# The last branch's operand kept in SBUF, the block combination moved into another stage, stores spread over three queues, and PSUM banks shared by stage

## The chip, the cores and the metric

One core of one Trainium2 chip runs the program. The metric is the device time of one execution in microseconds (us). The time before is 1762.13 us, the median of 3 runs (1758.29 to 1766.15).

A core has five engines with a queue each: PE (matmul, with its weight loads shown as PEld), DVE (vector), ACT (scalar functions), POOL and SP. They work side by side and wait for each other through semaphores; each queue is worked off in order. DMAs between the memories are started from a queue, which may have to wait there for the data that it is to store or for the buffer that it is to fill. Everything behind that DMA on the queue then waits as well. Matmuls write to PSUM, which has eight banks of 128 x 512 float32.

## The reference

One decoder block on x (1024 tokens, 1024 features), in float32: an RMSNorm, one wide projection that feeds three branches (a chunked gated delta rule, stick-breaking attention, attention on 256 memory tokens), a gated merge, an output projection with the residual, and a last RMSNorm.

```python
proj = rmsnorm(x, norm_g) @ w_in
dn_qkv, dn_z, dn_b, dn_a, sb_qkv, sb_z, m_q, m_z, gates = split(proj)
dn_qkv = silu(causal_dwconv(dn_qkv, conv_w))
o_dn = gated_delta_rule(l2norm(dq) * 128**-0.5, l2norm(dk), dv, beta, g)
o_dn = merge_heads(rmsnorm(o_dn, dn_norm_g)) * silu(dn_z)
o_sb = merge_heads(stick_breaking_attention(sq, sk, sv)) * silu(sb_z)
o_m = merge_heads(memory_attention(mq, mk, mv)) * silu(m_z)
g_dn, g_sb, g_m = split(sigmoid(gates), 3)
merged = g_dn * (o_dn @ w_br_dn) + g_sb * (o_sb @ w_br_sb) + g_m * (o_m @ w_br_mem)
out = rmsnorm(x + merged @ w_out, final_g)
```

The delta rule keeps a 128 x 128 state S for each of 8 heads; for each chunk it needs the inverse of a unit triangular matrix.

## The kernel before

**Arithmetic.** Each float32 operand of a large matmul is split into a high part (rounded by ACT) and a low part (the rest, by DVE; `split`, L136). A product is three matmuls: high·high, high·low, low·high (`mm3`, L150).

**The dense projection.** `stream` (L164) walks a list of jobs. A job is a pair of 128-feature groups for all 1024 tokens, done as a block product with seven multiplications instead of eight: units B11, B21, T1, T2, T3, B22, T4, of 12 matmuls each, 84 in all. Its four weight blocks are loaded from SP into `wb` (6 tiles); T units are differences of them, made by DVE. Each unit is split into `wu` (6 units ahead). The products gather in three kinds of bank, Y (two), X and Z (one each). A job's `evac` is called with each quarter of the result. One step of the generator, one unit, is called a *slot*, seven to a job. Slots are interleaved by hand with other work: `pacer` (L829) runs a second generator so far that its share of pieces matches the share of slots that have gone by.

**Order.** The program is written in order; the framework then plans each engine's queue by that order and by a simulated timeline, so neighbouring pieces can change places.

1. Norm (L254 to L358): x and mem are loaded, squared with a sum (ACT), scaled by the root and the gain in one DVE operation (L263), transposed by PE, split.
2. kq: eight jobs for k and q of the delta rule, four for the gate `sz`. `kq_head` (L473) convolves, and stores `kt`, `qd`, `kd`, `at`, `md`, `mo` for each half of a head; POOL masks the decay table `gam` (L482), clears the pads of `xp` (L457) and makes the row factors.
3. v (7 jobs: v and sv in turn) and z (10 jobs: mq, then dz and g in turn, mz). Beside them runs `solver` (L642), which inverts the 64 x 64 blocks on DVE: 62 elimination steps of two operations (L671, L674) on M, for all heads and chunks at once, then stores of the blocks (L680, L687). It has 80 pieces over the 119 slots of v and z. `memory` (L692) runs from z on. `stored` (L430) writes gates and z's through two staging tiles `st`.
4. Attention (L920 to L1007): `weights` makes z, two sigmoids, masks and a product scan (L942); `values` (L958) transposes and splits the weights, then multiplies by V. Between its pieces run the slots of skq and of the other eight gate jobs. `z` has one bank.
5. Merge (from L1018): `branch` (L1052) multiplies an operand with 128 columns of a branch's weights, gates the product and adds it to `mer`: first `ym` (8 times, 2 operand tiles), then `ysb` (8 times, 8 tiles). Beside these two run `combine` (L732), which joins pairs of 64-blocks into 128-blocks by two small products per head, and `recurrence` (L758), 16 steps (8 chunks, 2 groups of 4 heads) of four pieces: 80 pieces over 40 calls. A step loads kt, vb, tt, kd, qd, at; multiplies k·S (L780), T·r (L788), o = q·S + a·v (L795, L796) and dS (L800); squares, scales and transposes o; and stores it to `odn_d` in DRAM. When all are done, `load_o` (L1038) loads `odn_d` and `zf_d` tile by tile through `raw` (two tiles) and `gt`, multiplies and splits them, and `ydn` runs (8 times), with `wout` loaded beside it.
6. Output (from L1099): merged @ w_out, residual, norm, store.

All DMAs are started from SP.

Of the kernel before, what the change touches and what calls it, by code (L numbers as in the profile page):

```python
# [25 lines left out]
SV = 0.45  # L26
# [10 lines left out]
def hybrid_block(ctx, tc, x, mem, norm_g, mem_norm_g, wq, wv0, wba, convw, a_log, dt_bias,  # L37
# [39 lines left out]
    open_psum("psA", tr=4)  # L77
# [176 lines left out]
    def norm(pool_, src, g_bc, nm):  # L254
        xt = pool_.tile([P, T], F32, tag="xt", bufs=3, name="xt_" + nm)
        sy.dma_start(out=xt, in_=src)
        xn = pool_.tile([P, T], F32, tag="xn", name="xn_" + nm)
# [33 lines left out]
    def memory_kv():  # L291
        kv = [mp_.tile([P, 2, 256], F32, name=f"kv{j}") for j in range(2)]
        for i in range(2):
# [4 lines left out]
            ve.tensor_copy(kv[0][:, i, :], o[:, 0:256])  # L298
# [7 lines left out]
        ve.tensor_copy(kv[1], o.rearrange("p (a b) -> p a b", a=2))  # L306
# [114 lines left out]
    open_psum("psC", tr=2, wk=2)  # L421
# [5 lines left out]
    def staged(nm):  # L427
        return st.tile([P, 512], F32, tag="st", bufs=2, name=nm)

    def stored(d, fn, nm, post=None):  # L430

        def evac(i, j, a, b):
# [10 lines left out]
            sy.dma_start(out=d[j][:, half(i)], in_=t)  # L443
# [29 lines left out]
    def kq_head(h):  # L473
# [18 lines left out]
        def chunks(i):  # L492
# [3 lines left out]
            sy.dma_start(out=chunked(kt_d, h, i), in_=kv)  # L496
# [5 lines left out]
            sy.dma_start(out=chunked(qd_d, h, i), in_=qd)  # L502
# [3 lines left out]
            for j, (src, ss) in enumerate(((kv, ssk[:, s]), (qv, eq[:, h, s]))):  # L506
# [4 lines left out]
                if j == 0:  # L511
# [3 lines left out]
                    sy.dma_start(out=chunked(kd_d, h, i), in_=kd)  # L515
# [10 lines left out]
            sy.dma_start(out=chunked(at_d, h, i), in_=ma[:, :, 1, :])  # L526
            for b in range(2):
                q = slice(b * 64, b * 64 + 64)
                sy.dma_start(out=md_d[b, h, s].rearrange("n j i -> j n i"), in_=ma[q, :, 0, q])
            sy.dma_start(out=mo_d[h, :, s, :], in_=ma[0:64, :, 0, 64:P])  # L530
# [30 lines left out]
    def v_heads(g):  # L561
        xps = {}

        def conv(j, i):
# [8 lines left out]
            sy.dma_start(out=chunked(vb_d, h, i), in_=vb)  # L573
# [15 lines left out]
    def sv_heads(g):  # L589
        def evac(i, j, a, b):  # L590
# [6 lines left out]
            for d, s in zip(sv_d, hl):  # L597
                sy.dma_start(out=d[h, :, i * 4:i * 4 + 4, :], in_=f(s))
# [7 lines left out]

    mq = {}
# [6 lines left out]
    def gates(n):  # L614

        return (PQ_G + n, f"g{n}", stored([g_d[(2 * n + j) // 8, (2 * n + j) % 8] for j in range(2)],
                                          AF.Sigmoid, f"g{n}"))

    def silu_out(first, n, d, nm, post=None):
        return (first + n, f"{nm}{n}", stored([d[2 * n + j] for j in range(2)], AF.Silu, f"{nm}{n}", post))  # L620
# [16 lines left out]
    mzj = [silu_out(PQ_MZ, 0, zm_d, "mz", twice_silu)]  # L637
    dzj = [silu_out(PQ_DZ, n, zf_d, "dz", twice_silu) for n in range(4)]
    gj = [gates(n) for n in range(12)]


# [50 lines left out]
    def memory():  # L692
# [3 lines left out]
        for h in range(4):  # L696
# [25 lines left out]
            for hf in range(2):  # L722
# [6 lines left out]
                sy.dma_start(out=om_d[h // 2, r0:r0 + 64, half(hf)], in_=t[r0:r0 + 64])  # L729
            yield  # L730

    def combine():  # L732
        s_ = ExitStack()
        vp = pool("comb", 2, side="right", stack=s_)
# [23 lines left out]
    def recurrence():  # L758
# [9 lines left out]
        for n in range(NT):  # L768
            for g in range(2):
# [57 lines left out]
    SOLVE, MEM, RECUR = 1 + 1 + 62 + 8 + 8, 4 * 5, 16 + 16 * 4  # L827
# [21 lines left out]
    add("v", [vj[0], svj[0], vj[1], svj[1], vj[2], svj[2], vj[3]])  # L849
    add("z", mqj + [dzj[0], gj[0], dzj[1], gj[1], dzj[2], gj[2], dzj[3], gj[3]] + mzj)  # L850
# [43 lines left out]
    def beside():  # L894
        solve((pos[0] - first) / total)
# [8 lines left out]
    mem_ = pacer(memory(), MEM)  # L904
    start2 = pos[0]

    def beside2():
        beside()
        mem_((pos[0] - start2) / 60.0)
# [3 lines left out]
    solve(2.0)  # L913
    m_st.close()
    open_psum("psD", z=1, tr=2, av=1)


    d_st = sub()
    dp = pool("D", 1, stack=d_st)
# [38 lines left out]
    def values(h, i, at, vt):  # L958
# [18 lines left out]
        for b in range(i + 2):  # L977
# [3 lines left out]
            pe.matmul(o, vh, ah[:, b, cs_], start=(b == 0), stop=False)  # L981
            pe.matmul(o, vh, al_[:, b, cs_], start=False, stop=False)  # L982
            pe.matmul(o, vl, ah[:, b, cs_], start=False, stop=(b > i))
# [35 lines left out]
    opool = pool("op", 1, stack=w_st)  # L1019
    mp = pool("merged", 1, stack=w_st)  # L1020
# [17 lines left out]
    def load_o(src, ks, nm, by=None, op_=None, bufs=12):  # L1038
        res = []
        for k in ks:  # L1040
            raw = fp.tile([P, T], F32, tag="raw", bufs=2, name=f"oraw_{nm}_{k}")
            sy.dma_start(out=raw, in_=src[k])
            if by is not None:
                z_ = fp.tile([P, T], F32, tag="gt", bufs=4, name=f"oz_{nm}_{k}")
                sy.dma_start(out=z_, in_=by[k])
                ve.tensor_tensor(out=raw, in0=raw, in1=z_, op=ALU.mult)
            o = tuple((op_ or opool).tile([P, T], F32R, tag=f"o{j}", bufs=bufs, name=f"o{j}_{nm}_{k}") for j in "hl")
# [4 lines left out]
    def branch(i, w, nm, oT, br, first, each=lambda: None):  # L1052
        gt_ = fp.tile([P, T], F32, tag="gt", bufs=4, name=f"gt_{nm}")
# [157 lines left out]
```

## Time and profile before

| | us |
|---|---|
| median of 3 runs | 1762.13 |
| the profiled execution | 1764.58 |
| its span, first to last instruction | 1762.9 |

The profile's second part cuts the span into 40 slices of 44 us; a digit is the busy share in tenths, PEclk the granted TensorE clock in tenths of full speed, DMA the busy share of 16 DMA engines.

```profile
PE   4899999999979986999899999999868999729998
DVE  5887888879999952456777777767744334444332
ACT  5567877765544663644455454544422212322021
POOL 1002112110000000000101110111200001200011
PEclk9999999999999997999999999999968999959999
DMA  6336557564342244233123222311288746665122
```

The stages lie at 0 to 85 us (norm), 85 to 347 (kq), 347 to 497 (v), 497 to 775 (z), 775 to 1286 (attention), 1286 to 1575 (ym, ysb and the recurrence), 1575 to 1666 (ydn) and on to the end (output). A matmul that follows another closely starts 0.23 us after it at full clock (128 x 512), though each is shown with 0.39 us; so a busy PE need not be a PE at its peak.

### The profile page before, as it was taken

Reading aid. Unit: us, or ns where it says so; the run is one execution under the profiler, and the core shown is the slowest. Engines: PE = TensorE matmul, PEld = TensorE weight load, DVE = VectorE, ACT = ScalarE, POOL = GpSimd, SP = SyncE. Lnnn points to the kernel's source line nnn. Section 1 sums busy time; section 2 is a strip of 40 time slices with the busy share of each in tenths; the row PEclk is TensorE's granted clock in tenths of the full one; section 3 lists DMA queues with packets and bytes.
Section 4 is the critical chain, followed back from the end, with each engine's and each line's share of the span. In section 5 each row is a group of like instructions: output and inputs, shape, how many; then the busy total and the mean of one; then the engine's idle time right before and its main releaser. Section 6 shows DMA issues by size and latency. Waiting matters only on the chain.

```text
span 1762.9 us, 23066 instructions
## 1 busy us (share of the span) xinstructions
PE 1574.6 (89%) x7963; PEld 1304.6 (74%) x7963; DVE 1165.1 (66%) x1828; ACT 838.8 (48%) x1890; POOL 169.4 (10%) x405
## 2 busy tenths in 40 slices
PE   4899999999979986999899999999868999729998
PEld 4887788888867764777787778778756888628786
DVE  5887888879999952456777777767744334444332
ACT  5567877765544663644455454544422212322021
POOL 1002112110000000000101110111200001200011
PEclk9999999999999997999999999999968999959999
DMA  6336557564342244233123222311288746665122
GB/s 224 113 102 205 147 149 206 148 190 125 120 132 66 96 90 102 84 108 114 61 81 112 77 78 91 102 61 43 72 229 241 233 157 203 221 225 170 36 91 77
DMA packets 181317, 228.27 MB, mean 129 GB/s; under 512 B 50768, under 2 KB 104272, under 8 KB 181072
## 3 DMA queue, kind: packets, MB, share of 16 engines
q1 hardware_dynamic: 181200, 226.80, 41.7%
q8 instruction: 63, 1.03, 0.3%
q14 instruction: 54, 0.44, 0.1%
HBM read 152.72 MB, written 74.02 MB: 129 GB/s over the span
## 4 chain that ended last, share of the span: by engine, by line
PE 71%; DVE 11%; DMA 7%; ACT 4%; issue 3%; SPq 2%; POOL 1%; DVEq 0%; POOLq 0%; ACTq 0%
PE mmY_g L154 2%; PE mmY_g L155 2%; PE mmY_g L156 2%; PE y_ysb L1061 2%; PE y_ysb L1063 2%; PE y_ysb L1062 2%; PE y_ydn L1061 2%; PE mmY_skq L154 2%; PE out L1119 2%; PE y_ydn L1062 2%; PE mmY_skq L156 2%; PE mmY_skq L155 2%; PE out L1117 2%; PE y_ydn L1063 2%; PE out L1118 2%
## 5 line engine op out<-in xcount | busy, mean ns | idle before, releaser
L942 DVE TENSOR_TENSOR_SCAN pf<-pf 128x512 f32<-128x512 f32 (+4 forms) x96 | 98.3, 1024 | 38.0 <-POOL pf L940 35.4
L1061 PE MATMUL y_ydn<-oh_dn,wh_ydn 128*128 128x512 f32 x128 | 50.9, 398 | 38.0 <-ACT wh_ydn L1033 38.0
L137 ACT ACTIVATE aTh<-aTp 128x512 fp32r<-128x512 f32 (+2 forms) x96 | 45.1, 496 | 55.0 <-PE aTp L968 49.0
L936 ACT ACTIVATE pf<-z 128x512 f32<-128x512 f32 (+4 forms) x96 | 46.5, 485 | 48.5 <-PE z L156 48.1
L982 PE MATMUL av<-aTl,vh 128*128 128x256 f32 (+1 forms) x160 | 48.5, 303 | 12.6 <-DVE aTl L138 12.6
L138 DVE TENSOR_TENSOR aTl<-aTp,aTh 128x512 fp32r<-128x512 f32 (+2 forms) x96 | 50.8, 541 | 12.8 <-ACT aTh L137 12.8
L138 DVE TENSOR_TENSOR wu_g_T<-wt_g_T,wu_g_T 128x512 fp32r<-128x512 f32 x48 | 33.1, 689 | 36.4 <-ACT wu_g_T L137 36.3
L1061 PEld LDWEIGHTS y_ydn<-oh_dn,wh_ydn 128*128 128x128 f32 x128 | 24.6, 192 | 43.6 <-ACT wh_ydn L1033 38.4
L945 DVE TENSOR_TENSOR pf<-be,pf 128x512 f32<-128x512 f32 (+4 forms) x96 | 53.4, 556 | 4.0
L1061 PE MATMUL y_ysb<-oh_sb,wh_ysb 128*128 128x512 f32 x128 | 52.0, 407 | 2.9 <-ACT wh_ysb L137 2.9
L674 DVE TENSOR_TENSOR M<-M,tmp 128x62 f32<-128x62 f32 (+30 forms) x62 | 52.7, 850 | 0.3
L671 DVE TENSOR_TENSOR tmp<-M 128x62 f32<-128x62 f32 (+30 forms) x62 | 52.7, 850 | 0.3
L1117 PE MATMUL out<-oh_wo,mh 128*128 128x512 f32 x128 | 50.3, 393 | 1.8 <-ACT mh L137 1.8
L1062 PE MATMUL y_ysb<-ol_sb,wh_ysb 128*128 128x512 f32 x128 | 51.6, 403 | 0.0
L1063 PE MATMUL y_ysb<-oh_sb,wl_ysb 128*128 128x512 f32 x128 | 51.5, 404 | 0.0
L1062 PE MATMUL y_ydn<-ol_dn,wh_ydn 128*128 128x512 f32 x128 | 50.6, 395 | 0.0
L1063 PE MATMUL y_ydn<-oh_dn,wl_ydn 128*128 128x512 f32 x128 | 50.3, 395 | 0.0
L1118 PE MATMUL out<-ol_wo,mh 128*128 128x512 f32 x128 | 50.3, 393 | 0.0
L1119 PE MATMUL out<-oh_wo,ml 128*128 128x512 f32 x128 | 49.7, 392 | 0.0
L154 PE MATMUL z<-kh,qh 128*128 128x512 f32 (+4 forms) x96 | 36.6, 381 | 14.3 <-ACT be L937 14.3
L940 POOL TENSOR_SCALAR_AFFINE_SELECT pf<-pf 128x128 f32<-128x128 f32 x64 | 22.8, 356 | 273.7 <-ACT pf L936 270.9
L137 ACT ACTIVATE wu_g_T<-wt_g_T 128x512 fp32r<-128x512 f32 x48 | 30.1, 630 | 38.7 <-PE mmY_g L156 11.9
(790 smaller groups left out, 5379.3 us busy)
## 6 DMA issues: line engine op xcount, KB each, us to landing
wb_g_b<-in_wq_dram SPq DMA_DIRECT2D x48, 256.0 KB
g_d<-g SPq DMA_DIRECT2D x48, 256.0 KB
wb_kq_b<-in_wq_dram SPq DMA_DIRECT2D x32, 256.0 KB
wb_skq_b<-in_wq_dram SPq DMA_DIRECT2D x32, 256.0 KB
xt_x<-in_x_dram SPq DMA_DIRECT2D x8, 512.0 KB
wb_sz_b<-in_wq_dram SPq DMA_DIRECT2D x16, 256.0 KB
kt_d<-kq SPq DMA_DIRECT2D x16, 256.0 KB
gam<-gr_d SPq DMA_DIRECT2D x8, 512.0 KB
```

The source lines that it names most:

```text
L137: sc.activation(dst[0], src, AF.Copy)
L138: ve.tensor_tensor(out=dst[1], in0=src, in1=f(dst[0]), op=ALU.subtract)
L154: pe.matmul(o, ah, bh, start=(first and i == 0), stop=False, **kw)
L155: pe.matmul(o, ah, bl, start=False, stop=False, **kw)
L156: pe.matmul(o, al, bh, start=False, stop=(i == n - 1), **kw)
L942: ve.tensor_tensor_scan(out=pv[:, ::-1], data0=pv[:, ::-1], data1=pv[:, ::-1], initial=pf[:, off + c1:off + c1 + 1], op0=ALU.mult, op1=ALU ...
L1061: pe.matmul(oo[hf], wh[:, k, :], oh[:, s], start=(k == 0), stop=False)
L1062: pe.matmul(oo[hf], wh[:, k, :], ol[:, s], start=False, stop=False)
L1063: pe.matmul(oo[hf], wl[:, k, :], oh[:, s], start=False, stop=(k == n - 1))
L1117: pe.matmul(oo[hf], mh[:, k, :], wo[k][0][:, s], start=(k == 0), stop=False)
L1118: pe.matmul(oo[hf], mh[:, k, :], wo[k][1][:, s], start=False, stop=False)
L1119: pe.matmul(oo[hf], ml[:, k, :], wo[k][0][:, s], start=False, stop=(k == KC - 1))
```

## The change

- *The last branch's operand.* The recurrence loads `zt`, its part of silu(dn_z), multiplies the transposed o with it and splits it into `odn`, two SBUF tensors of 128 x 8 x 1024. `odn_d`, its stores and loads go. To make room, `kd`, `qd`, `at` have one buffer instead of two, the branch weights two instead of three, the gates are loaded by halves into two half tiles (four whole ones before), operands have 8 buffers (12), and `om`'s multiplier goes through `raw`.
- *Combine.* It runs in z, from 72% of the slots of v and z to 98%, after the solver, whose pieces are spread over those 72%; it has single buffers.
- *Jobs.* v: v and g in turn (four each), then three sv. z: mq, four dz, mz. `memory` is spread over 32 slots instead of 60. The first four gates are made with tanh on ACT and a POOL operation.
- *Queues.* On ACT: kt, sz, vb, om, gates from the fifth on. On POOL: qd, kd, at, md, mo, sv, dz, mz, the first four gates. Staging has three tiles.
- *Banks.* X has a bank of its own only in kq, v and z; in attention it shares two banks with z. The norm has five banks for transposes.
- *Norm.* POOL multiplies by the gain, ACT scales by the root.
- *Attention.* `values` begins with the blocks whose weights were split first. Three slots run between `memory` and the first attention piece.

```diff
-    MM = dict(Y=2, X=1, Z=1)
+    MM = dict(Y=2, Z=1)
     def psum(tag, name):
+        if tag == "X" and "X" not in banks["tags"]:
+            tag = "z"
...
         sc.activation(xn, xt, AF.Square, accum_out=ss)
+        gp.tensor_tensor(out=xt, in0=xt, in1=g_bc, op=ALU.mult)
...
-        ve.scalar_tensor_tensor(out=xt, in0=xt, scalar=rs, in1=g_bc, op0=ALU.mult, op1=ALU.mult)
-        return xt
+        sc.activation(xn, xt, AF.Copy, scale=rs)
+        return xn
...
-    open_psum("psC", tr=2, wk=2)
+    open_psum("psC", tr=2, wk=2, X=1)
...
-            sy.dma_start(out=d[j][:, half(i)], in_=t)
+            q.dma_start(out=d[j][:, half(i)], in_=t)
...
-            sy.dma_start(out=chunked(qd_d, h, i), in_=qd)
+            gp.dma_start(out=chunked(qd_d, h, i), in_=qd)
...
+    def sigmoid(t, src, nm):
+
+        sc.activation(t, src, AF.Tanh, scale=0.5)
+        gp.tensor_scalar(out=t, in0=t, scalar1=0.5, scalar2=0.5, op0=ALU.mult, op1=ALU.add)
...
-                kd = ld(kd_d, n, g, "kd") if n < NT - 1 else None
-                qd = ld(qd_d, n, g, "qd") if n else None
-                at = ld(at_d, n, g, "at")
+                kd = ld(kd_d, n, g, "kd", 1) if n < NT - 1 else None
+                qd = ld(qd_d, n, g, "qd", 1) if n else None
+                at = ld(at_d, n, g, "at", 1)
+                zt = ep.tile([P, 4, P], F32, tag="zt", bufs=1, name=f"zt_{n}_{g}")
+                sy.dma_start(out=zt, in_=zf_d[g * 4:g * 4 + 4, :, n * P:n * P + P].rearrange("h d t -> d h t"))
...
-                os_ = ep.tile([P, 4, P], F32, tag="os", bufs=2, name=f"os_{n}_{g}")
-                sc.activation(os_, o.rearrange("p (h c) -> p h c", h=4), AF.Copy)
-                sy.dma_start(out=odn_d[g * 4:g * 4 + 4, :, n * P:n * P + P].rearrange("h d c -> d h c"), in_=os_)
+                ve.tensor_tensor(out=zt, in0=o.rearrange("p (h c) -> p h c", h=4), in1=zt, op=ALU.mult)
+                split([t[:, g * 4:g * 4 + 4, n * P:n * P + P] for t in odn], zt)
...
-    add("v", [vj[0], svj[0], vj[1], svj[1], vj[2], svj[2], vj[3]])
-    add("z", mqj + [dzj[0], gj[0], dzj[1], gj[1], dzj[2], gj[2], dzj[3], gj[3]] + mzj)
+    add("v", [vj[0], gj[0], vj[1], gj[1], vj[2], gj[2], vj[3], gj[3]] + svj)
+    add("z", mqj + dzj + mzj)
...
     def beside():
-        solve((pos[0] - first) / total)
+        solve((pos[0] - first) / (SF * total))
...
-        mem_((pos[0] - start2) / 60.0)
+        mem_((pos[0] - start2) / 32.0)
+        if pos[0] - first > SF * total:
+            solve(2.0)
+            comb((pos[0] - first - SF * total) / ((0.98 - SF) * total))
...
-    open_psum("psD", z=1, tr=2, av=1)
     d_st = sub()
     dp = pool("D", 1, stack=d_st)
+    for _ in range(3):
+        slot()
+    open_psum("psD", z=2, tr=2, av=1)
...
-        for b in range(i + 2):
+        bs = list(range((i + 1) // 2 if i >= 4 else 0, i + 2)) + (list(range((i + 1) // 2)) if i >= 4 else [])
+        for m, b in enumerate(bs):
...
-    recur = pacer(itertools.chain(combine(), recurrence()), RECUR)
+    recur = pacer(recurrence(odn), RECUR)
...
-        w = [fp.tile([P, T], F32R, tag=f"w{j}", bufs=3, name=f"w{j}_{nm}") for j in "hl"]
+        w = [fp.tile([P, T], F32R, tag=f"w{j}", bufs=2, name=f"w{j}_{nm}") for j in "hl"]
...
-                z_ = fp.tile([P, T], F32, tag="gt", bufs=4, name=f"oz_{nm}_{k}")
+                z_ = fp.tile([P, T], F32, tag="raw", bufs=2, name=f"oz_{nm}_{k}")
...
+        if i < 6:
+            osb += load_o(osb_d, [i], "sb")
         branch(i, tuple(t_[:, (i % 4) * 2:(i % 4) * 2 + 2, :] for t_ in wm), f"ym_{i}", oT, 2, True, beside3)
-        osb += load_o(osb_d, [i], "sb")
+    osb += load_o(osb_d, (6, 7), "sb")
...
-    odn = load_o(odn_d, range(8), "dn", zf_d)
+    dT = [tuple(t[:, k, :] for t in odn) for k in range(H)]
```

More of the change, by code (lines that the diff above doesn't have):

```diff
@@ L25 @@
 NB, NS, NU = 6, 3, 6
-SV = 0.45
+SF = 0.72
 RP = 1.05
@@ L612, in mq_evac, with gates, silu_out @@
         put(mq[j][:, half(i)], a, b)
[L614 removed]
+    def gates(n, post=None, q=sc):
         return (PQ_G + n, f"g{n}", stored([g_d[(2 * n + j) // 8, (2 * n + j) % 8] for j in range(2)],
[L617 to L620 removed]
+                                          AF.Sigmoid, f"g{n}", post, q))
+    def silu_out(first, n, d, nm, post=None, q=sc):
+        return (first + n, f"{nm}{n}", stored([d[2 * n + j] for j in range(2)], AF.Silu, f"{nm}{n}", post, q))
     def lazy(fn, *args):
@@ L636, in hybrid_block @@
     mqj = [(PQ_MQ, "mq", mq_evac)]
-    mzj = [silu_out(PQ_MZ, 0, zm_d, "mz", twice_silu)]
-    dzj = [silu_out(PQ_DZ, n, zf_d, "dz", twice_silu) for n in range(4)]
-    gj = [gates(n) for n in range(12)]
+    mzj = [silu_out(PQ_MZ, 0, zm_d, "mz", twice_silu, gp)]
+    dzj = [silu_out(PQ_DZ, n, zf_d, "dz", twice_silu, gp) for n in range(4)]
+    gj = [gates(n, sigmoid, gp) for n in range(4)] + [gates(n) for n in range(4, 12)]
     def solver():
@@ L904, in hybrid_block @@
     mem_ = pacer(memory(), MEM)
+    comb = pacer(combine(), COMB)
     start2 = pos[0]
@@ L1019, in hybrid_block @@
     opool = pool("op", 1, stack=w_st)
+    dpool = pool("dn", 1, stack=w_st)
+    odn = [dpool.tile([P, H, T], F32R, name=f"odn{j}") for j in "hl"]
     mp = pool("merged", 1, stack=w_st)
@@ L1052, in branch @@
     def branch(i, w, nm, oT, br, first, each=lambda: None):
-        gt_ = fp.tile([P, T], F32, tag="gt", bufs=4, name=f"gt_{nm}")
-        sy.dma_start(out=gt_, in_=g_d[br, i])
+        gt_ = []
+        for hf in range(2):
+            gt_.append(fp.tile([P, 512], F32, tag="gt", bufs=2, name=f"gt_{nm}_{hf}"))
+            sy.dma_start(out=gt_[hf], in_=g_d[br, i, :, half(hf)])
         wh, wl = w
```

57 lines of the change are left out of this document (28 added, 29 removed).

## The prediction

> **What bounds the kernel now.** I read the page's first two parts, then the busy time of each engine in stretches cut at the stage borders, then PE's waits in each stretch, then the chain of waits and the queue's timeline where PE stood still.
>
> ```profile
> span 1762.9 us, 23066 instructions
> PE 1574.6 (89%) x7963; PEld 1304.6 (74%) x7963; DVE 1165.1 (66%) x1828; ACT 838.8 (48%) x1890; POOL 169.4 (10%) x405
> ```
>
> ```profile
> 85.00:346.70 261.70, 254.84 (x1252) 212.07 (x1252) 216.48 (x358) 194.83 (x536) 45.12 (x76) 1.00 0.54 157
> 346.70:497.00 150.30, 148.73 (x715) 123.38 (x714) 139.41 (x216) 90.08 (x204) 7.43 (x18) 1.00 0.48 144
> 497.00:620.00 123.00, 111.23 (x478) 85.52 (x479) 117.94 (x165) 66.19 (x143) 5.74 (x8) 0.94 0.30 96
> 620.00:690.00 70.00, 46.83 (x181) 32.57 (x180) 25.37 (x48) 35.40 (x65) 1.48 (x4) 0.83 0.46 96
> 820.00:1287.00 467.00, 432.67 (x2259) 363.86 (x2257) 340.83 (x525) 232.96 (x484) 64.58 (x190) 0.99 0.24 78
> 1287.00:1365.00 78.00, 54.72 (x354) 44.74 (x355) 36.58 (x42) 19.89 (x22) 0.00 (x0) 0.72 0.89 254
> 1365.00:1496.00 131.00, 130.33 (x784) 114.58 (x783) 49.66 (x114) 27.01 (x99) 13.20 (x27) 1.00 0.59 195
> 1496.00:1577.00 81.00, 35.09 (x263) 31.50 (x262) 37.37 (x69) 25.99 (x79) 10.25 (x21) 0.74 0.70 230
> ```
>
> After the colon each row has the length, the busy time of PE, PEld, DVE, ACT and POOL with counts, PE's granted clock, the DMA share and GB/s. PE is the bound: 89% busy, and full from 85 to 497 and from 1365 to 1496. It loses time in four places: v and z (DVE is 96% busy from 497 to 620, and PE idles 23 us from 620 to 690), attention (34 us idle in 467), the opening of the merge (23 us idle, the clock down to 0.72, the DMAs 89% busy), and the end of the recurrence (46 us idle, clock 0.74).
>
> ```profile
> PE y_ydn L1061 <- ACT wh_ydn L1033: 38.0, 1, 38.0
> PE mmY_g L154 <- ACT g L440: 20.2, 1, 20.2
> ACT L440 <- DMA g_d<-g: 18.3, 1, 18.3
> PE z L154 <- ACT be L937: 14.3, 18, 1.1
> PE av L982 <- DVE aTl L138: 12.6, 16, 1.3
> PE Y L743 <- DMA ct<-mo_d: 13.7, 1, 13.7
> ```
>
> ```profile
> 649.08 14.62 SPq L687 DMA_DIRECT2D tt_d<-M  x6
> ```
>
> The second and third rows are one event: SP stood on six of the solver's stores for 14.6 us, the gate's store waited behind them, its staging tile stayed taken, ACT could not empty PE's bank, and PE idled 20.2 us. The first row is the last branch's operand on its way through DRAM:
>
> ```profile
> 1378.62 0.89 PE Tr L788 x8
> 1486.06 0.91 PE Tr L788 x8
> 1505.98 3.38 DMA tt<-tt_d
> 1522.94 1.26 PE Tr L788 x8
> 1527.20 0.24 PE o L796 x2
> 1535.22 4.64 DMA oraw_dn<-odn_d
> 1568.12 5.77 DMA raw_ydn<-in_wbd_dram
> 1575.11 0.80 PE y_ydn L1061
> ```
>
> From the recurrence's last product (1527) to the first of `y_ydn` (1575) PE waits for four rounds of load, multiply and split, and then for the branch's first weights, whose `raw` buffer those loads held.
>
> **The change part by part.** The sum is against the profiled execution, 1764.58 us around a span of 1762.9; the median of the runs is 1762.13, 2.4 below.
>
> *The merge stage, 1286 to 1575: 289 us.* Rows for the terms:
>
> ```profile
> 1286.01 0.41 PE L983 MATMUL av<-aTh,vl 128*128 128x128 f32 x1
> 1308.88 0.79 PE L1061 MATMUL y_ym<-oh_m,wh_wbm 128*128 128x512 f32 x1
> 1340.70 4.61 DMA oraw_sb<-osb_d
> 1345.34 1.07 ACT oh_sb L137
> 1346.43 1.24 DVE ol_sb L138
> 1351.26 1.14 PE L750 MATMUL X<-t,Ys 64*64 64x64 f32 x16
> 1470.22 0.23 PE y_ysb L1061
> ```
>
> (a) Opening: `om`, `zm` and the first weights now pass through two shared `raw` slots. Before, `ym` began 23 us after attention's end, held up by loads; now 6 us for the first pair, then `om` and `zm` of k = 1, multiplied, then `wbm`, each a load of 4.6 us plus about 1.2: I keep 23. (b) `ym`: ten more tiles go through the two slots up to the first weights of `ysb`. A slot's turn is 4.61 + 1.07 + 1.24 = 6.9 us, so 3.5 us a tile, 35 us; `osb` 6 and 7 and the weights behind them wait until `ym` lets go of its two operand buffers, two turns in series: 48 us in all. About 3.4 of 16 recurrence steps fit in, by the pacer (8 of 40 calls, times 1.05, of 64 pieces). (c) `ysb`: 384 matmuls of 0.23 us, 88, with the other 12.6 steps. A step has 37 products of 0.11 us on average (0.89 for 8), 4.1, and its transposes 0.4: 57 us. Together 145. (d) The tail: one step alone, then its squares, POOL's three operations, the scaling, the transposes, and the new multiply and split, about 12 us; the first four heads of `ydn`, 5 us, lie beside it. 23 + 48 + 145 + 12 = 228: **61 us less**. Of that, 18 is `combine` (256 products of 1.14/16), which comes back in z. Removed for good are the stores of `odn_d`, its loads and the splits. Added on DVE per step are a multiply and a subtract of 0.69, 22 us in all, hidden while DVE is busy 50 of 131 us; were that cover gone they would cost the 22. `zt` adds 4 MB where 8 MB of `odn_d` and `zf_d` loads go. `kd`, `qd`, `at` with one buffer make SP wait for the step's products; queued behind on SP are the next step's loads and the branch weights. Lower end of that cost nothing, upper end 3.4 us (a load of `tt` as above) in 16 steps, 54 us; I take nothing, since the steps beside `ysb` are 11 us apart and a load takes a third of that.
>
> *v and z, 346.7 to 775.*
>
> ```profile
> L154 PE MATMUL mmY_skq<-hA11h,wu_skq_B x32: 389/391/496, 775.0 to 1191.6; 128*128 128x512 f32 x32
> L674 DVE TENSOR_TENSOR M<-M,tmp 128x62 f32<-128x62 f32 (+30 forms) x62 | 52.7, 850 | 0.3
> L671 DVE TENSOR_TENSOR tmp<-M 128x62 f32<-128x62 f32 (+30 forms) x62 | 52.7, 850 | 0.3
> L138 DVE TENSOR_TENSOR wu_g_T<-wt_g_T,wu_g_T 128x512 fp32r<-128x512 f32 x48 | 33.1, 689 | 36.4 <-ACT wu_g_T L137 36.3
> L451 DVE SCALAR_TENSOR_TENSOR y_v<-xp_v,cw,y_v 128x512 f32<-128x512 f32 x48 | 35.0, 742 | 1.4 <-POOL xp_v L457 1.4
> ```
>
> `combine` adds 18 us of PE. The 20.2 us gap goes: `dz` and the first gates are stored from POOL, the staging has three tiles. What is late next there is the weight loads, still on SP behind the solver's stores and now also behind `combine`'s; six raw tiles are 1.5 jobs, about 29 us of cover against a block of 14.6. The solver's 105.4 us of DVE moves forward: its last elimination step was due in slot 95 of 119 and is now due in slot 69. A job's slot needs 84 × 0.23 / 7 = 2.8 us of PE; DVE needs 14 operations of 0.69 (11 in conversions, 3 in evacuation) a job, 1.4 a slot, and 2.7 with a convolution (12 × 0.74 more). So DVE has about 1.1 us to spare in a mean slot, and 26 fewer slots would cost 28 us. But the last step had ended by 631.6, when the stores of M begin (row of L687 below): 285 of 428 us, about slot 79 of 119, ahead of its pace. From there to 69 is 10 slots, 11 us. Bounds 0 and 28, taken 11. Sum +18 − 20 + 11 = **+9**.
>
> *Attention.* Two banks for `z`: while X holds one (four slots of seven) nothing changes, so three sevenths of 14.3, 6 us. The new order of blocks needs only the first half's low part, one ACT and one DVE operation earlier: I take 8 of 12.6. X now waits for a free `z` bank: +2. **−12** (bounds −25 and +5).
>
> *Norm and kq.* POOL multiplies by the gain, DVE's scaling goes to ACT. The trace has no two-input POOL operation this wide:
>
> ```profile
> L482 POOL TENSOR_SCALAR_AFFINE_SELECT gam<-gam x8: 1104/1460/2142, 126.0 to 348.9; 128x1024 f32<-128x1024 f32 x8
> L687 SPq DMA_DIRECT2D tt_d<-M x16: 324/1550/4220, 631.6 to 674.1; - x16
> q1 hardware_dynamic: 181200, 226.80, 41.7%
> ```
>
> One-input operations of that size take up to 2.14, and the DVE ones that go would be a gain where DVE was late: bounds −3 and +10 (ten tiles, 1 us longer each), taken **+2**. The Trainium skill (GPSIMD Engine Reference, 3.1 Elementwise) has 4497 ns for a two-input operation of 2048 elements; an estimate of 2.25 us for ours by that page would also come to +2, and no run here shows it. Stores from ACT cost its queue 0.32 us each at least (the shortest issue of L687), 32 of them in kq beside 195 us busy in 262: nothing; without that cover they would add 10. Stores from POOL in kq: one DMA costs between 0.32 and 4.22 us by the row of L687 (median 1.55), which I take; bounded below.
>
> Total: −61 + 9 − 12 + 2 = −62: 1764.6 − 62 = 1702.6. **Forecast 1703 us**, own range 1680 to 1722.
>
> **The rivals.**
>
> *POOL becomes the bound in kq (slower).* A head there has 261.7 / 8 = 32.7 us. POOL computes 45.1 / 8 = 5.6 of it, and now starts 12 stores a head (`qd`, `kd`, `at`, `md`, `mo`), whose chunked targets are many short rows. Behind them on POOL wait the next head's `gam` mask, the pads of `xp` and the row factors, for which ACT, then DVE, then PE wait. POOL decides from (32.7 − 5.6) / 12 = 2.26 us a store. At 3.1 (twice the median) a head takes 42.8, 81 us more in all: 1784. For it: the long issues of L687. Against: the shortest of that row is 0.32, and the long ones stood in a row on one queue. The Trainium skill (DMA: Bandwidth & Descriptors, SWDGE vs HWDGE vs iDMA) says that software on GpSimd writes the descriptors of its DMAs, hardware those of SP and ACT; it would make this rival likelier. By the q1 row the kernel had hardware queues alone, so nothing here shows it. 14%.
>
> *DVE becomes the bound in v.* The solver follows its new pace to the letter and its chain holds the evacuations: +28 instead of +11, and `combine`'s single buffers stop PE at each of eight heads for about 2 us of load: 1736. For it: DVE 96% busy where the solver runs now. Against: it already ran ahead of its pace. 16%.
>
> *The recurrence does not fit beside `ysb`.* The single buffers cost 3.4 us in most steps, the steps lie bare after `ysb`, as seven do now (`Tr` from 1486 to 1523, 6.2 us apart): half to all of the 54 us, 1730 to 1757, taken as 1745. For it: the same rows of `tt`. 12%.
>
> *More than forecast.* Steps are drawn into the idle PE of `ym`, attention loses all its waits, DVE is no later than now: 1672. 12%.
>
> **How the numbers follow.** 46% for the forecast. 0.5% is about what a measurement of this kernel can tell from no change: 1753 and 1771. Below 1753 lie the forecast, the better case, DVE's rival and half of the recurrence's: 46 + 12 + 16 + 6 = 80%; the other half is within, 6%; POOL's is above, 14%. The range leaves out POOL's rival and half of the better one: 1668 to 1758.
>
> **What would show it.** Right: no wait of some 38 us before the first `y_ydn`, and 10 us or less from the last `o` product to it; 220 to 240 us from attention's last `av` to `y_ydn`; no 20 us gap at `mmY_g`; the first `mmY_skq` at about 785; waits of `z` on `be` and of `av` on `aTl` halved. Wrong: the kq stretch well over 265 us with `gam` or `xp` waited for; `mmY_skq` after 800 with DVE full up to the solver's end; a row of `kS`, `Tr` and `o` alone after the last `y_ysb`, or PE waiting for weights between `ym` and `ysb` for longer than 10 us.

## The result, and the profile after

| | us | ratio to before (95% interval) |
|---|---|---|
| before, median (1758.29 to 1766.15) | 1761.91 | |
| changed, median (1675.41 to 1678.40) | 1677.89 | 0.952 (0.9496 to 0.9543) |
| changed, the profiled execution | 1678.14, span 1676.4 | |

The change makes the kernel 84 us faster. The forecast was 1703, the range 1668 to 1758: the time lies inside, 25 us below the forecast. The first part of the page after:

```profile
span 1676.4 us, 23005 instructions
PE 1559.0 (93%) x7963; PEld 1299.6 (78%) x7963; DVE 1168.0 (70%) x1831; ACT 817.2 (49%) x1877; POOL 314.6 (19%) x587
```

PE has as many matmuls as before and is busy 16 us less, but the span is 86 shorter: what went is mostly idle time. Where it went shows when the span is cut at the first matmul of each stage (`mmY_kq`, `mmY_v`, `y_ydn`, `out`) and at the last `av`, in us. The three stages on which the experiments turn are v to `av` (v, z and attention), the merge, and `ydn`:

| | norm | kq | v to last `av` | to `y_ydn` | to `out` | to the end |
|---|---|---|---|---|---|---|
| before | 85.1 | 261.6 | 939.3 | 289.1 | 89.3 | 98.5 |
| changed | 93.2 | 261.9 | 917.7 | 204.5 | 103.3 | 95.8 |
| difference | +8.1 | +0.3 | −21.6 | −84.6 | +14.0 | −2.7 |

Busy time by stretch after, in the columns of the prediction's table (length; PE, PEld, DVE, ACT, POOL; clock, DMA share, GB/s):

```profile
768.00:1273.00 505.00, 497.03 (x2658) 415.60 (x2656) 369.22 (x579) 271.40 (x581) 72.95 (x204) 0.99 0.28 87
...
1283.00:1355.00 72.00, 61.80 (x385) 54.70 (x385) 49.54 (x98) 28.34 (x83) 9.85 (x21) 0.93 0.96 330
1355.00:1477.00 122.00, 121.20 (x683) 105.30 (x684) 59.52 (x115) 26.58 (x80) 10.82 (x22) 1.00 0.57 186
1477.00:1580.00 103.00, 97.85 (x454) 81.91 (x453) 44.19 (x63) 19.64 (x35) 3.05 (x7) 0.97 0.40 127
```

Attention now leaves PE 8 us idle in 505; before it left 34 idle in the 467 us of the prediction's row. The merge's opening moves 330 GB/s where it moved 254. The same view for the `Tr` products alone, eight to a step of the recurrence, shows where its 16 steps lie (length; PE, PEld and ACT; clock, DMA share, GB/s):

```profile
1283.00:1355.00 72.00, 10.06 (x64) 8.94 (x64) 4.37 (x8) 0.93 0.96 330
1355.00:1477.00 122.00, 6.99 (x48) 6.61 (x48) 4.00 (x7) 1.00 0.57 186
1477.00:1580.00 103.00, 2.11 (x16) 2.02 (x16) 1.21 (x2) 0.97 0.40 127
```

Eight steps start before the first `y_ysb` (1355), three of them in the opening, six beside `ysb` and two beside `ydn`; before, eight started beside `ysb` and eight after its last product (1485.7). The PE timeline shows no pause where it waited 38.0 us:

```profile
1477.04 0.39 PE L1084 MATMUL y_ysb<-oh_sb,wl_ysb 128*128 128x512 f32 x1
1477.27 0.39 PE L1082 MATMUL y_ydn<-odnh,wh_ydn 128*128 128x512 f32 x1
```

PE's longest waits after (total, times, longest), the first in z, the next two in attention, the last in the merge's opening:

```profile
PE mmZ_dz L156 <- DVE dz L246: 24.3, 2, 18.7
...
PE z L156 <- ACT be L952: 0.7, 1, 0.7
PE av L999 <- DVE aTl L140: 1.5, 2, 0.9
...
PE Tr L798 <- DMA tt<-tt_d: 10.4, 1, 10.4
```

The waits of `z` and `av` have gone (14.3 and 12.6 before). The gap in z has not: it is 24.3 where it was 20.2, on another tile. SP's queue (start, us, DMA, count) says why:

```profile
636.80 5.06 SPq L149 DMA_DIRECT2D wb_dz_b<-in_wq_dram  x3
643.99 0.77 SPq L695 DMA_DIRECT2D tt_d<-M  x2
645.13 5.61 SPq L688 DMA_DIRECT2D t_d<-T  x2
650.79 16.46 SPq L695 DMA_DIRECT2D tt_d<-M  x6
667.35 0.87 SPq L688 DMA_DIRECT2D t_d<-T  x1
668.27 17.04 SPq L695 DMA_DIRECT2D tt_d<-M  x8
685.41 3.83 SPq L149 DMA_DIRECT2D wb_dz_b<-in_wq_dram  x3
```

For 41 us SP starts nothing but the solver's stores (`tt_d`, and `t1_d`, shown as `t_d`), and the next weights of z leave at 685. The gates no longer stand behind them, the weights do.

### The profile page after: what moved, and what is told of

Read it like the earlier page. It is cut to its first block, busy times and chain, and to the rows that moved or that the text cites. A ratio compares the mean times of both kernels' runs of the same rounds, so it can differ in the third digit from the quotient of the medians.

```text
span 1676.4 us, 23005 instructions
## 1 busy us (share of the span) xinstructions
PE 1559.0 (93%) x7963; PEld 1299.6 (78%) x7963; DVE 1168.0 (70%) x1831; ACT 817.2 (49%) x1877; POOL 314.6 (19%) x587
## 4 chain that ended last, share of the span: by engine, by line
PE 78%; DVE 7%; DMA 5%; issue 4%; SPq 3%; ACT 3%; POOL 1%; ACTq 0%; DVEq 0%; POOLq 0%
PE mmY_g L156 3%; PE mmY_g L158 3%; PE mmY_g L157 3%; SPq L695 2%; PE mmY_skq L156 2%; PE aTp L983 2%; PE mmY_skq L158 2%; PE mmY_skq L157 2%; PE out L1141 2%; PE out L1139 2%; PE mmY_kq L156 2%; PE out L1140 2%; PE mmY_kq L158 2%; PE y_ysb L1084 2%; PE mmY_kq L157 2%
## 5 line engine op out<-in xcount | busy, mean ns | idle before, releaser
L1082 PE MATMUL y_ydn<-odnh,wh_ydn 128*128 128x512 f32 x128 | 50.0, 395 | 0.0
L1083 PE MATMUL y_ydn<-odnl,wh_ydn 128*128 128x512 f32 x128 | 49.7, 389 | 0.0
L1084 PE MATMUL y_ydn<-odnh,wl_ydn 128*128 128x512 f32 x128 | 49.6, 390 | 0.0
L952 ACT ACTIVATE be<-z 128x512 f32<-128x512 f32 (+4 forms) x96 | 47.4, 503 | 4.4 <-DVE pf L960 4.4
L998 PE MATMUL av<-aTh,vh 128*128 128x256 f32 (+1 forms) x160 | 44.6, 279 | 1.7 <-ACT aTh L139 1.7
L1000 PE MATMUL av<-aTh,vl 128*128 128x256 f32 (+1 forms) x160 | 45.4, 283 | 0.0
L1146 DVE TENSOR_TENSOR xo<-out,xo 128x512 f32<-128x512 f32 x16 | 11.1, 692 | 48.0 <-PE out L1141 48.0
```

The lines of the kernel that those rows point to most:

```text
L1082: pe.matmul(oo[hf], wh[:, k, :], oh[:, s], start=(k == 0), stop=False)
L1083: pe.matmul(oo[hf], wh[:, k, :], ol[:, s], start=False, stop=False)
L1084: pe.matmul(oo[hf], wl[:, k, :], oh[:, s], start=False, stop=(k == n - 1))
```

## The experiments

Each is an edit of the changed kernel (1677.9); differences are to that median, stage lengths are cut as in the table above.

**The operand through DRAM again.**

```diff
-                zt = ep.tile([P, 4, P], F32, tag="zt", bufs=1, name=f"zt_{n}_{g}")
-                sy.dma_start(out=zt, in_=zf_d[g * 4:g * 4 + 4, :, n * P:n * P + P].rearrange("h d t -> d h t"))
...
-                ve.tensor_tensor(out=zt, in0=o.rearrange("p (h c) -> p h c", h=4), in1=zt, op=ALU.mult)
-                split([t[:, g * 4:g * 4 + 4, n * P:n * P + P] for t in odn], zt)
+                os_ = ep.tile([P, 4, P], F32, tag="os", bufs=1, name=f"os_{n}_{g}")
+                sc.activation(os_, o.rearrange("p (h c) -> p h c", h=4), AF.Copy)
+                sy.dma_start(out=odn_d[g * 4:g * 4 + 4, :, n * P:n * P + P].rearrange("h d c -> d h c"), in_=os_)
...
+    for k in range(H):
+        raw = fp.tile([P, T], F32, tag="raw", bufs=2, name=f"draw_{k}")
+        sy.dma_start(out=raw, in_=odn_d[k])
+        z_ = fp.tile([P, T], F32, tag="raw", bufs=2, name=f"dz_{k}")
+        sy.dma_start(out=z_, in_=zf_d[k])
+        ve.tensor_tensor(out=raw, in0=raw, in1=z_, op=ALU.mult)
+        split([t[:, k, :] for t in odn], raw)
```

> The changed kernel (1677.9 us) with one part undone: the recurrence stores its output to DRAM again, and after it the last branch's operand is loaded, multiplied and split, into the same SBUF tensors. Theory A (the trip through DRAM is a serial wait ahead of the last branch, 48 us before, of which some 8 stay in the changed kernel): PE idle of 35 to 45 us ahead of the first y_ydn is back, 1713 to 1723 us. Theory B (the gain came from the recurrence starting earlier, the trip would now be hidden beside it): less than 15 us, under 1693.

Measured 1737.71, +60 (ratio to before 0.987, 0.984 to 0.990): theory A in kind, 15 us above its range. PE's wait, and the busy time of the stretch after the last `y_ysb`:

```profile
PE y_ydn L1081 <- ACT wh_ydn L1051: 58.8, 1, 58.8
```

```profile
1476.00:1550.00 74.00, 9.48 (x66) 8.14 (x66) 24.45 (x27) 14.65 (x30) 2.93 (x6) 0.59 0.46 152
```

All of the 60 comes from this one place, where PE works 9.5 us in 74: the merge is 72 us longer, and `ydn` 13 shorter, since no steps are left to run beside it. The way through DRAM costs more here than in the kernel before (a wait of 58.8 against 38.0). A likely reason is that the gate's part passes through the same two `raw` tiles here, so that 16 loads take turns in two slots; that was not tried. So 60 us is what undoing this part costs in the changed kernel; the part that the kernel before paid is nearer to its own wait of 38.

**Combine back into the merge.**

```diff
...
-            comb((pos[0] - first - SF * total) / ((0.98 - SF) * total))
...
-    recur = pacer(recurrence(odn), RECUR)
+    recur = pacer(itertools.chain(combine(), recurrence(odn)), COMB + RECUR)
```

> The changed kernel with combine put back ahead of the recurrence in the merge stage, all else as it is. Theory A (in the merge's opening, which waits for loads, combine takes the place of the recurrence steps that are drawn there; z loses combine's 18 us of PE): the merge stage is 35 to 45 us longer, v to attention 15 to 20 shorter, 1693 to 1708 us. Theory B (the opening has room for both, only the place changes): within 8 us of 1678.

Measured 1685.89, +8.0 (ratio 0.957, 0.954 to 0.960). By its time it lies at the edge of theory B, but the mechanism is theory A's: two large amounts nearly cancel. From v to `av` the time falls from 917.7 to 884.4 (−33), and the merge with `ydn` grows from 307.8 to 354.6 (+47); the rest is the norm (89.3 instead of 93.2). So `combine`, 18 us of products by its row before, costs 33 in z and attention and 47 in the merge. Of the 33, 23 are busy time of PE and 10 idle: the wait of 24.3 at `mmZ_dz` isn't there without `combine`, and smaller ones of `memory` are. The 47 can't be added to the 60 of the edit before: together they are more than the 71 us by which the merge with `ydn` shrank (378.4 to 307.8). Why the merge pays so much, the listings of its products and of `Tr` show (first and last start):

```profile
L758 PE MATMUL X<-t,Ys x128: 218/218/366, 1249.2 to 1331.3; 64*64 64x64 f32 x128
...
L798 PE MATMUL Tr<-vb,tt x128: 272/275/377, 1342.0 to 1495.7; 128*128 128x128 f32 x128
```

The recurrence waits until `combine` has ended (1331). No step lies before `ysb`, and eight are left for after it, so that `ydn` takes 145 us instead of 103.

**The banks.**

```diff
-    MM = dict(Y=2, Z=1)
+    MM = dict(Y=2, X=1, Z=1)
     def psum(tag, name):
-        if tag == "X" and "X" not in banks["tags"]:
-            tag = "z"
...
-    open_psum("psC", tr=2, wk=2, X=1)
+    open_psum("psC", tr=2, wk=2)
...
-    open_psum("psD", z=2, tr=2, av=1)
+    open_psum("psD", z=1, tr=2, av=1)
```

(and the norm's five transpose banks back to four.)

> The changed kernel with the banks of before (X a bank of its own throughout, one bank for z in attention, four for the norm's transposes). Theory A (X holds a bank too short to matter, so a second z bank takes away all of the waits of z on the sigmoids, 14.3 us, and 4.6 of mmZ): 1693 to 1699 us, with these waits back. Theory B (the forecast's step: X holds one of two banks for four slots of seven, so 6 us of 14.3 less 2 for X): 1680 to 1684 us.

Measured 1720.83, +43 (ratio 0.978, 0.976 to 0.979), more than either theory had. It lies in attention, 548 us for 505; the other stages differ by 5 us at most and cancel. The stretch from its first product to its last, and PE's two longest waits there:

```profile
768.00:1316.00 548.00, 515.21 (x2655) 423.34 (x2653) 373.43 (x579) 271.52 (x580) 72.53 (x203) 0.97 0.26 80
```

```profile
PE av L997 <- DVE aTl L138: 12.4, 17, 1.3
PE z L154 <- ACT be L950: 8.0, 10, 1.1
```

For the same number of matmuls (within 3) PE idles 33 us instead of 8, and is shown busy 18 us longer. That is 25 + 18 = 43. The named waits add up to some 32, against some 8 with two banks, so they tell of the 25 alone; the 18 are matmuls that are shown longer (likely their gaps, shown as busy). The `av` waits come back with the bank, though the new order of blocks is still there.

**The order of blocks in `values`.**

```diff
-        bs = list(range((i + 1) // 2 if i >= 4 else 0, i + 2)) + (list(range((i + 1) // 2)) if i >= 4 else [])
+        bs = list(range(i + 2))
```

> The changed kernel with the order of the blocks in values as before, from block 0 up. Theory A (the wait of av on the second half's low part, 12.6 us before and 1.5 in the changed kernel): 1686 to 1690 us, with that wait back at about 12 us. Theory B (with two z banks PE has other work to put there, so the order no longer matters): within 4 us of 1678.

Measured 1675.27, −2.6 (ratio 0.952, 0.950 to 0.953): nothing, as theory B had it. With two `z` banks `av` doesn't wait in either order.

**All DMAs from SP** (each `gp.dma_start`, `sc.dma_start`, `q.dma_start` becomes `sy.dma_start`).

> The changed kernel with every DMA started from SP again. Theory A (the stores on SP hold up the loads and through the staging tiles PE, as the 20 us gap before showed): 1693 to 1705 us, with PE waiting on ACT or DVE behind stores of gates and dz. Theory B (the gap in z has the same length whichever queue stores, since the solver's stores block SP in both): within 6 us of 1678.

Measured 1682.13, +4.2 (ratio 0.955, 0.953 to 0.957). kq takes 263.8 for 261.9, and the gap in z stays (23.6), as theory B had it. The spread over three queues is worth a few microseconds at most.

**The norm on DVE, as before.**

```diff
-        gp.tensor_tensor(out=xt, in0=xt, in1=g_bc, op=ALU.mult)
-        sc.activation(xn, xt, AF.Copy, scale=rs)
+        ve.scalar_tensor_tensor(out=xt, in0=xt, scalar=rs, in1=g_bc, op0=ALU.mult, op1=ALU.mult)
```

(with three tiles of x instead of two, and one for the squares instead of two.)

> The changed kernel with the norm of before: DVE scales by root and gain in one operation, three tiles of x and one for the squares. Theory A (POOL's multiplies of 2.4 us stand ahead of the root in its queue and hold back the first transposes, 17.4 us in place of 11.3, and the first kq product, 93 in place of 85): 1668 to 1672 us. Theory B (the delay comes from the loads of x, which stand later in the queue): within 3 us of 1678.

Measured 1669.69, −8.2 (ratio 0.948, 0.947 to 0.950): the first `mmY_kq` comes at 83.2 instead of 93.2. In the other edits that keep the changed kernel's norm it comes at 89.3 to 92.5, so 93.2 is its upper end. POOL's multiplication in the changed kernel, and PE's wait for the first normalised tile there:

```profile
L262 POOL TENSOR_TENSOR xt_x<-xt_x,g x8: 2347/2396/2730, 25.0 to 75.6; 128x1024 f32<-128x1024 f32 x8
```

```profile
PE xT_m L275 <- ACT xn_m L266: 17.4, 1, 17.4
```

Before, that wait was 11.3 us: the pair of operations stands in the chain to PE's first work, where DVE was not late.

**The jobs of v and z in the old order.**

```diff
-    add("v", [vj[0], gj[0], vj[1], gj[1], vj[2], gj[2], vj[3], gj[3]] + svj)
-    add("z", mqj + dzj + mzj)
+    add("v", [vj[0], svj[0], vj[1], svj[1], vj[2], svj[2], vj[3]])
+    add("z", mqj + [dzj[0], gj[0], dzj[1], gj[1], dzj[2], gj[2], dzj[3], gj[3]] + mzj)
```

> The changed kernel with the job lists of before (v and sv in turn, then mq, dz and g in turn, mz). Theory A (the solver's 240 us on a full DVE are there in any order; what counts is how many jobs PE gets through in them, 69 slots now and 63 before, since gates cost DVE less than sv): about 17 us slower, 1690 to 1698 us, with the solver's last step still 235 to 250 us after its first. Theory B (the solver's new pace made the stage shorter): within 5 us of 1678.

Measured 1665.68, −12.2 (ratio 0.946, 0.943 to 0.948): both theories fall, the new order is the worse one. v to `av` takes 907.6. The same SP block stands here from 645 to 685, but the gap is 14.9. ACT's timeline in it (idle before and its releaser in brackets):

```profile
663.46 0.59 ACT L736 ACTIVATE mot<-mo 64x512 f32<-64x512 f32 x1 [3.72 <-PE mo L733]
679.66 0.45 ACTq L737 DMA_DIRECT2D om_d<-mot  x1
680.22 0.60 ACT L612 ACTIVATE g<-mmY_g 128x512 f32<-128x512 f32 x1 [16.16 <-DMA tt_d<-M]
```

Here the weights were in time, and it is ACT's own store of `om` that got through only when SP's were nearly done. What it waited for is a landing. In this program all DMAs from SP and ACT announce their landing on eight semaphores, used in turn, and a DMA waits until the one before it on its semaphore has landed. The semaphore of `om`'s store still belonged to a store of M that SP started at 673.05; it landed at 679.59, and ACT's store started at 679.66. The Trainium skill (Perfetto Trace Analysis, DMA Instruction — HWDGE (DVE, Sync)) says that two issuing sequencers share one block that generates descriptors, and lock it in turn. These 16 us are no case of that: they end with the landing, and the store itself is shown with 0.45 us.

**The solver's stores from POOL.**

```diff
-                sy.dma_start(out=tt_d[:, q, h, q], in_=M[s])
+                gp.dma_start(out=tt_d[:, q, h, q], in_=M[s])
```

(and its four stores of `t1_d`.)

> The changed kernel with the solver's 20 stores started from POOL instead of SP. Theory A (PE's wait of 18.7 us at mmZ_dz comes from the weight loads, which stand on SP behind 35 us of these stores): the wait is gone, 1656 to 1663 us. Theory B (the wait belongs to the dz jobs and their staging): no change, 1675 to 1681 us. Theory C (POOL stands on the stores as SP did and holds up the maxima and the dz stores behind them): a wait of the same length in another place, 1675 us or more.

Measured 1734.15, +56 (ratio 0.985, 0.982 to 0.988): theory C, but with a wait four times as long. POOL's queue, the median from issue to landing of its stores of M (the last figure), and the waits:

```profile
643.34 0.94 POOL L695 DMA_DIRECT2D tt_d<-M  x1 [13.92 <-DVE M L682]
649.12 0.82 POOL L695 DMA_DIRECT2D tt_d<-M  x1 [4.83 <-issue]
654.73 0.81 POOL L695 DMA_DIRECT2D tt_d<-M  x1 [4.79 <-issue]
...
729.36 1.69 POOL L446 DMA_DIRECT2D zf_d<-dz  x3
```

```profile
tt_d<-M POOLq DMA_DIRECT2D x16, 128.0 KB, 5.2
```

```profile
PE mmX_dz L156 <- ACT dz L243: 80.7, 1, 80.7
ACT dz L243 <- DMA zf_d<-dz: 79.4, 1, 79.4
```

Each of these stores holds POOL for some 5.5 us from start to start (2.1 to 2.7 on SP), 86 us in all. That is about the time to its landing: the first landed at 648.70, and the next was started at 649.12. Behind them stand the stores of `dz`, so the three staging tiles stay taken, ACT can't empty PE's bank, and PE idles 80.7 us. It is the prediction's chain of before, with POOL in SP's place: on both queues that were tried, something that PE needs stands behind these stores. So the next edit changes the stores.

**M stored in one piece.** A store of before writes 8 partitions x 64 rows of 64 numbers: 512 rows of 256 bytes. Now M leaves in its own order, and a step of the recurrence gathers its block with three loads; `combine` reads and writes arrays of its own, and the eight stores of zeros go.

```diff
-        for h in range(H):
-            for b in range(2):
...
-                sy.dma_start(out=tt_d[:, q, h, q], in_=M[s])
+        sy.dma_start(out=tb_d.rearrange("b h n k r -> (b h n) k r"), in_=M)
...
-                tt = ld(tt_d, n, g, "tt")
+                tt = ep.tile([P, 4, P], F32, tag="tt", bufs=2, name=f"tt_{n}_{g}")
+                gp.memset(tt[64:P, :, 0:64], 0.0)
+                for b in range(2):
+                    q = slice(b * 64, b * 64 + 64)
+                    sy.dma_start(out=tt[q, :, q], in_=tb_d[b, g * 4:g * 4 + 4, n].rearrange("h k r -> k h r"))
+                sy.dma_start(out=tt[0:64, :, 64:P], in_=x_d[n, :, g * 4:g * 4 + 4, :])
```

> Edit of the changed kernel: the solver's M leaves in one store, in its own order (128 rows of 16 KB), instead of 16 stores of 512 rows of 256 bytes; combine's block has an array of its own; a recurrence step reads tt in three loads (two of 256 short rows, one of 64 rows of 1 KB) and POOL clears the zero quarter. Theory A (it is the 16 stores' many short rows that hold SP from 644 to 685, and behind them the weights of z): SP is free by about 665, the 24 us wait of mmZ_dz falls below 5, first v product to last av 918 -> about 897; the merge pays little since a step's loads have 8 to 11 us: 1660 (1652 to 1668). Theory B (the gap has other makers, the solver's end on DVE or the bytes): the wait stays, and the short rows, moved into the recurrence, cost SP about 2 us in each of 16 steps, most of it in the opening where the DMAs are 96% busy: 1680 to 1712.

Measured 1655.33, −22.6 (ratio 0.941, 0.938 to 0.943), within theory A's range. SP's queue, and the busy time of the 60 us in which PE stood before:

```profile
637.98 0.33 SPq L688 DMA_DIRECT2D tb_d<-M  x1
639.10 1.85 SPq L685 DMA_DIRECT2D t_d<-T  x2
643.90 0.33 SPq L150 DMA_DIRECT2D wb_dz_b<-in_wq_dram  x1
```

```profile
640.00:700.00 60.00, 60.00 (x308) 45.19 (x306) 33.10 (x55) 29.59 (x63) 5.58 (x12) 1.00 0.48 149
```

The same row of the changed kernel:

```profile
640.00:700.00 60.00, 35.69 (x143) 28.11 (x142) 23.39 (x40) 11.78 (x21) 3.31 (x6) 0.77 0.52 111
```

PE no longer stands, and its clock is 1.00 where it was 0.77. v to `av` falls by 30.7 to 887.0; the merge pays 5.5 (210.0). The one store carries the bytes of all sixteen in 0.33 us of SP's time, so it was the form of the sixteen stores and not their bytes. It wasn't the number of short rows alone. In the changed kernel, `combine` stores its block into the same array with as many rows of the same length, but from 64 partitions instead of 8, and one at a time (shortest, median and longest in ns):

```profile
L695 SPq DMA_DIRECT2D tt_d<-M x16: 341/1868/4336, 644.0 to 683.5; - x16
...
L761 SPq DMA_DIRECT2D tt_d<-Xs x8: 586/590/633, 706.8 to 840.7; - x8
```

Such a store holds SP for 0.59 us. The first two stores of M hold it for 0.34 and 0.38, and only those behind them for more; the two `t_d` stores among them, with 64 rows of 4 KB, take 2.8 each there and 0.9 here. This fits an SP that is held by what hasn't yet gone through ahead. While it stood (644 to 685), the 16 DMA engines were 49% busy and moved 90 GB/s; in the 10 us after the one store started, 92% and 338 GB/s. The edit changes the rows, the partitions that a store reads and the number of stores together, and no run tells these apart.

**Putting together.** First norm, job order and block order of before:

> Edit of the changed kernel: norm, job order and order of the attention blocks as before the change, together. Theory A (each of the three has its own place and they add up): -8.2 - 12.2 - 2.6 = -23: 1655 (1650 to 1660), first mmY_kq at about 83, first v product to last av about 908. Theory B (the gain of the job order was in part the norm's spread, 89.6 against 93.0 to the first mmY_kq, and comes only once): 1659 to 1665.

Measured 1665.44 (ratio 0.946, 0.943 to 0.949): no better than the old job order alone (1665.68). The gains don't add up, against theory A; kq takes 265.9 here and PE waits 13.3 us for one of `combine`'s loads. Why kq grows was not tried. Then the same three with M in one piece:

> Edit: norm, job order and block order of before the change, and M stored in one piece, together. Theory A (short rows hold the queues in z whatever the order of jobs; here ACT's store of om and behind it the gates stood behind them, 15 us): about 13 to 18 under the kernel without the single store, 1640 (1633 to 1648). Theory B (the single store only moves the cost into the recurrence): the same as without it or slower, 1655 to 1680.

Measured 1641.53 (ratio 0.932, 0.930 to 0.935), as theory A had it. And these without the old job order (norm, block order and M in one piece):

> Edit: norm and block order of before the change and M stored in one piece, with the changed kernel's own job order. Theory A (the 12 us that the old job order gained lay in what stood behind the short rows: a 15 us wait there instead of 24; with one long store nothing stands, so the orders are alike): 1641 to 1646, as with the old order (1641.5), ratio to before about 0.932. Theory B (the old order gains by the mix of gates and z's jobs, whatever the stores): some 10 above it, 1650 to 1655, ratio about 0.938.

Measured 1642.54 (ratio 0.934, 0.931 to 0.936). With the sixteen stores gone the two orders are alike, as theory A had it. That the 12 us of the job order lay in who stood behind those stores is shown only in part: with the norm of before, the old order was worth some 4 us even with them (1669.69 to 1665.44, the second with the old block order too). The last two kernels are the fastest, 36 us below the change and 120 below the kernel before.

## Why the prediction was right, and where not

The time lies within the range, but nearer to the rival "more than forecast" (1672, 12%) than to the forecast (1703). Of that rival's three conditions two came: steps were drawn in beside `ym`, and attention's waits went. The third, a DVE no later than before, came nearly: the solver ended 4 us later.

- *The operand in SBUF* was right in kind: there is no wait before `y_ydn`. Undoing it costs 60 us. The prediction counted PE's pause before it from 1527, 48 us; the recurrence's last transpose runs until 1537, and PE's own wait there was 38.0.
- *The merge, −61 forecast, −84.6 measured, of which `ydn` gives back 14.* Term by term: opening 23, measured 26.3 (1272.8 to 1299.1); `ym` 48, measured 55.9; `ysb` 145, measured 122.0; tail 12, measured 0.3. The step mis-sized is the one that let only 3.4 steps fit into `ym` by the pacer: eight had started by its end, three of them in the idle PE of the opening, so `ysb` carried six and not 12.6. The time from the last `av` to `y_ydn`, 204.5, fell below the 220 to 240 that were to show the forecast right. The edit with `combine` in front of the recurrence (no step there, eight left over) shows that it is `combine`'s leaving that opens the place. The tail was wrong in form: the last two steps don't stand alone, `ydn` runs beside them. The rival "more than forecast" had named the drawn-in steps.
- *The single buffers at nothing*: PE waits 4.9 us for one `qd`, 2.1 for a `kd` and 1.0 for an `at`, no more; the rival by which the recurrence doesn't fit did not happen.
- *v and z, +9, and attention, −12: together −3 forecast, −21.6 measured.* Most of the terms were wrong in size. `combine` was taken as its 18 us of products and cost 33. The gap at `mmY_g` (−20) did not go, though the step after it was right: "late next there is the weight loads" is what the profile shows; the cover of 29 us was held against a block of 14.6, while the whole block is 41. The solver's 11 us did not come: its last step ends 289 us after the first product of v (644.0 − 355.1), where it had ended 285 after it, so it was not drawn forward at all. And two banks for `z` were to help in three sevenths of the time, 6 − 2 = 4 us; they were worth 43 to 47. This is the step that was furthest off: X's use of a bank hardly held `z` up (it waits 0.7 us in all), and the named waits didn't hold the whole price. The new order of blocks, 8 us, was worth nothing once they were there. That the sum of this stretch came out on the right side is partly luck: the banks' gain covers what `combine` and the gap cost against the forecast. The runs leave about −18 of it without an owner (the rest after `combine` +33, banks −47, job order +10, block order −1, queues +1); staging, `memory`'s pace and the tanh gates were not tried singly.
- *The norm, +2, measured +8.* The wait in front of PE was taken as mostly hidden; the trace shows that it is not, and the edit that undoes it gains 8.2. The bound of 10 held.
- *POOL's rival, 14%.* It decided from 2.26 us a store, and POOL's stores of kq take:

```profile
L518 POOL DMA_DIRECT2D kd_d<-kd x16: 762/847/882, 128.6 to 372.6; - x16
...
L532 POOL DMA_DIRECT2D md_d<-ma x32: 628/632/650, 136.7 to 376.5; - x32
```

kq is as long as before. The mechanism exists, but in z, and only with the solver's stores: at 5.5 us each they make PE wait 80.7 us and the kernel 56 us longer. That the rival's price was 81 too is chance.

By stage, the merge with `ydn` gave 71 us for 61, v to `av` 22 for 3, and norm and kq cost 8 for 2; the sum was 25 us short, and most of that lies in v to `av`, where the account was wrong.

## What to carry to other kernels

A block of many stores, each with short rows out of few partitions, can hold the queue that issues them, and moving it, or what stands behind it, to another queue only changed the victim here: look at the form of each store and at what waits behind it, and store the tile at once in its own order where the reader can gather. A PSUM bank's worth need not be the sum of the waits named on it. Where work is moved out of a place, ask what stood behind it: `combine` was small, but the recurrence waited for it.

## What the runs showed of the hardware

- The time that a store holds its queue follows neither its bytes nor its rows alone. On SP it was 0.33 us for 2 MB in 128 rows of 16 KB; 0.59 for 128 KB in 512 rows of 256 bytes from 64 partitions; and 2.1 to 2.7 for as much in as many rows from 8 partitions, sixteen nearly in a row. On POOL it was 5.5 for the last kind, of which only 0.8 is shown as the instruction and the rest as idle for "issue"; a `kd` store (512 rows of 512 bytes from 128 partitions) took 0.8 there.
- Stores of M from 8 partitions, issued one after the other on SP, left the 16 DMA engines 49% busy at 90 GB/s; one store of all 128 partitions had them 92% busy at 338 GB/s. That a store from few partitions uses only some of the engines would fit; no run tests it.
- The Trainium skill (DMA: Bandwidth & Descriptors, Issuing engines are not separate DMA queues) says that starting DMAs from several engines saves only the time to start them, usually small. The spread over three queues agrees with it (4.2 us). For the solver's stores the time is not small, 41 us on SP, and starting them on POOL instead made the kernel 56 us longer.
